# A fused two-block transformer kernel: the first modulation's products in turns with the norm's square sums, and the first dense tile in turns with the gates' products

## The chip, the cores and the metric

One core of a Trainium2 chip runs the whole program. The metric is the device time of one execution in microseconds, the median of three runs; lower is better. The engines are TensorE (PE in the rows; PEld is its weight loads), VectorE (DVE), ScalarE (ACT), GpSimd (POOL) and SyncE (SP), whose queue starts nearly all loads.

## The reference

Two blocks follow each other on 256 tokens of width 1024; the change lies in the first forty to seventy microseconds, at the start of the first block:

```python
mod = jax.nn.silu(c) @ w_ada[l] + b_ada[l]                  # 1024 -> 6 x 1024
sh1, sc1, g1, sh2, sc2, g2 = jnp.split(mod, 6, axis=-1)
h = modulate(x, norm1_g[l], sh1, sc1)                       # rms_norm(x, g) * (1 + sc1) + sh1
proj = h @ w_in[l]
q_a, k_a, v_a, qk_m, v_m, o_m, gates = jnp.split(proj, offs, axis=-1)
qa = rope(split_heads(q_a, ATT_HEADS), positions)           # sines and cosines of the positions
...
qk_m = jax.nn.silu(causal_conv(qk_m, conv_w[l], conv_b[l]))
gates = gates.astype(jnp.float32) + b_gate[l].astype(jnp.float32)
...
hm = mlstm_chunkwise(..., i_pre, f_pre)                     # uses the gates and qk_m, v_m
y = jnp.concatenate([attn.astype(x.dtype), hm], axis=-1) @ w_out[l]
x = x + g1[:, None, :] * y
...                                                         # 32 experts, then the second block
```

## The kernel before

Activations lie transposed: a tile is 128 features by 256 tokens, and `xT`, `hT` are eight of them. A dense product (`dense_t`) loads 1 MB of weights into a tile `w`, splits each half into a rounded part `whi` (ScalarE, line 267) and a rest `wlo` (VectorE, line 268), does the same to the activations (`hh`, `hl`), and adds three products for each of 8 feature blocks (`mm3`): 24 matmuls for a half, 48 for a whole block. All matmuls come from line 280.

The function `first` begins with the norm (`rstd`: ScalarE squares a block of `xT` into a tile `ats`, TensorE sums it over the features), then the sines and cosines of the positions (`sincos`: eleven short operations on VectorE and ScalarE from the load `posi`), then the modulation (`ada`): eight loads of 1 MB of `wada`, each with four matmuls against `crep`, a copy `m` on ScalarE, four transposes and one addition into `mod`. Three groups of `mod` are made; group 0 is needed at once, groups 1 and 2 (`more`) are taken one step after each dense block. From `mod` come `a1` and, block by block, `hh`, `hT` and `hl`; then the gates' products (`wg` against `hT`, eight matmuls of 36 columns of weights), the function `gates`, and four dense blocks for `qk_m`, each copied from the PSUM to a tile `raw` and then convolved.

The order on each engine isn't the order of the code. A scheduler works it out when the program is built, from the order of the code, the buffers that are free and its own estimate of each instruction's time; each engine then executes its list in that order. `tc.issue_after(x)` puts the instructions that are written under it, on the engine of `x`, behind `x`, without a wait on a semaphore. What limits the scheduler here: the pool `raw` holds five 1 MB tiles `w`, so a sixth load starts only when the first is used; the pool of `whi` and `wlo` holds four halves of each; `ps` has two PSUM banks, and one of them is held by the modulation group under way (`psum_banks(ps=2, at=3, ml=2, kv=1)`).

Of the kernel before, what the change touches and what calls it, by code (L numbers as in the profile page):

```python
# [3 lines left out]

# [1 line left out]

# [9 lines left out]
AF = mybir.ActivationFunctionType  # L16
OP = mybir.AluOpType
# [164 lines left out]
def bc(ap, n):  # L182

    return ap[:, None, :].to_broadcast([ap.shape[0], n, ap.shape[1]])
# [23 lines left out]
class Kern:  # L208
# [55 lines left out]

    def split(self, src, hi, lo, eng=None):

        self.nc.scalar.activation(hi, src, AF.Copy)  # L267
        (eng or self.nc.vector).tensor_sub(lo, src, hi.bitcast(F32))  # L268
        return hi, lo

# [6 lines left out]
            yield self.split(raw[:, 1024 * i:1024 * i + 1024], hi, lo, self.nc.gpsimd if i < self.spread else None)  # L277

    def mm(self, ps, l, r, start, stop, **kw):
        self.nc.tensor.matmul(ps, l, r, start=start, stop=stop, **kw)  # L280

    def mm3(self, ps, l, r, start, stop, **kw):

        self.mm(ps, l[0], r[0], start, False, **kw)
        self.mm(ps, l[0], r[1], False, False, **kw)
        self.mm(ps, l[1], r[0], False, stop, **kw)

    def dense_t(self, src, act, other=iter(())):

# [70 lines left out]
    def sincos(self, pool, ang, n, tag, tmp=None, out=None):  # L360

        nc = self.nc
        MAGIC = 12582912.0
        c1 = 6.28125
        c2 = float(np.float32(np.round((2 * PI - c1) * 2 ** 21) / 2 ** 21))
        c3 = float(np.float32(2 * PI - c1 - c2))
        k, r = (self.t(tmp[0], [128, n], tmp[1]) if tmp else self.t(pool, [128, n], tag + i) for i in "kr")
        s, c = out or [self.t(pool, [128, n], tag + i) for i in "sc"]
        nc.vector.tensor_scalar(k, ang, 1.0 / (2 * PI), MAGIC, op0=OP.mult, op1=OP.add)
        nc.vector.tensor_scalar(k, k, MAGIC, None, op0=OP.subtract)  # L370
        nc.vector.scalar_tensor_tensor(r, k, -c1, ang, op0=OP.mult, op1=OP.add)
        nc.vector.scalar_tensor_tensor(r, k, -c2, r, op0=OP.mult, op1=OP.add)
        nc.vector.scalar_tensor_tensor(r, k, -c3, r, op0=OP.mult, op1=OP.add)
        lim = 3.1415925
        nc.vector.tensor_scalar(r, r, -lim, lim, op0=OP.max, op1=OP.min)
        nc.scalar.activation(s, r, AF.Sin)
        nc.vector.scalar_tensor_tensor(k, r, -1.0, r, op0=OP.mult, op1=OP.max)
        nc.scalar.activation(c, k, AF.Sin, bias=self.halfpi, scale=-1.0)
        return s, c


# [22 lines left out]
    def ada(self, pool, g, crep):  # L404

        nc = self.nc
        ps = self.psum()
        for k in range(8):
            w = self.load(self.io["wada"][g, k])
            for j in range(4):  # L410
                self.mm(ps[32 * j:32 * j + 32], crep[:, k], w[:, 512 * j:512 * j + 512], k == 0, k == 7)
            yield
        m = self.t(pool, [128, 512], "ats")
        nc.scalar.activation(m, ps, AF.Copy)
        pt = self.psum().rearrange("p (q j r) -> p j q r", q=4, j=4)
        for q in range(4):
            nc.tensor.transpose(pt[:, :, q].rearrange("p j r -> p j r"), m[:, 128 * q:128 * q + 128], self.ident)
        dst = self.mod[:, 16 * g:16 * g + 16].rearrange("p (j q) -> p j q", j=4)
        b = self.v("b_ada", 16 * g, 16).rearrange("p (j q) -> p j q", j=4)
        nc.vector.tensor_add(dst, pt[:, :, :, 0], b)  # L420
# [16 lines left out]
    def first(self, M):  # L437
        nc, io, tc = self.nc, self.io, self.tc
        with tc.tile_pool(name="p1", bufs=1) as P, tc.tile_pool(name="p1w", bufs=2) as W:
            sc = self.t(P, [128, 8], "sc")  # L440
            nc.scalar.activation(sc, self.v("c"), AF.Silu)
            crep = self.t(P, [128, 8, 32], "crep")
            nc.vector.tensor_copy(crep, sc[:, :, None].to_broadcast([128, 8, 32]))
            C = self.load_c(P, ["cmask", "tneg", "rot", "hsel", "invf"])

            r1, _ = self.rstd(W, self.xT, "cv", sq="ats")
            hT = self.slot(0).rearrange("p (a b) -> p a b", a=8)
            nc.vector.tensor_mul(hT, self.xT, bc(r1, 8))
            posi = self.t(W, [128, T], "cv", I32)
# [13 lines left out]
            nc.vector.tensor_copy(ang, posi)  # L463
            nc.vector.tensor_scalar(ang, ang, C["invf"], None, op0=OP.mult)
            self.sincos(P, ang, T, "rp", (W, "cv"), (sinT, cosT))
            for _ in self.ada(W, 0, crep):
                pass
            more = itertools.chain(self.ada(W, 1, crep), self.ada(W, 2, crep))
            a1 = self.t(P, [128, 8], "a1")
            nc.vector.scalar_tensor_tensor(a1, self.m(1), 1.0, self.v("norm1_g"), op0=OP.add, op1=OP.mult)  # L470
            hh = self.t(P, [128, 8, T], "hh", F32R)
            hl = self.t(P, [128, 8, T], "hl", F32R)
            for k in range(8):
                nc.scalar.activation(hh[:, k], hT[:, k], AF.Identity, bias=self.mod[:, k:k + 1], scale=a1[:, k:k + 1])
                nc.vector.tensor_scalar(hT[:, k], hT[:, k], a1[:, k:k + 1], self.mod[:, k:k + 1], op0=OP.mult, op1=OP.add)
                nc.vector.tensor_sub(hl[:, k], hT[:, k], hh[:, k].bitcast(F32))
            h = (hh, hl)
            self.out("h", hT)
            wg = self.t(P, [128, 8, 36], "wg")
            nc.sync.dma_start(wg, io["wgate"][0])  # L480
            bg = self.t(P, [36, 1], "bg")
            nc.sync.dma_start(bg, io["bgate"])
            pg = self.psum("ml")[0:36, :T]
            for k in range(8):
                self.mm(pg, wg[:, k], hT[:, k], k == 0, k == 7)
            self.gates(P, C, pg, bg, hn, so)

            qkm = self.slot(1).rearrange("p (a b) -> p a b", a=8)
            for b in (0, 2, 1, 3):
                ps = self.dense_t(io["win"][4 + b], h)  # L490
                next(more, None)
                raw = next(raws)
                nc.scalar.activation(raw, ps, AF.Copy)
                for c in range(2):
                    f = 2 * b + c
                    cv = qkm[:, f]
                    wc = self.v("conv_w", 4 * f, 4)
                    nc.vector.tensor_scalar(cv, raw[:, c], wc[:, 3:4], self.v("conv_b", f), op0=OP.mult, op1=OP.add)
                    for d in (1, 2, 3):
                        nc.vector.scalar_tensor_tensor(cv[:, d:], raw[:, c, :T - d], wc[:, 3 - d:4 - d], cv[:, d:],  # L500
                                                       op0=OP.mult, op1=OP.add)
                if b >= 2:
                    for x in (qkm[:, 2 * b - 4:2 * b - 2], qkm[:, 2 * b:2 * b + 2]):
                        nc.scalar.activation(x, x, AF.Silu)
                    nc.gpsimd.tensor_scalar(x, x, 128.0 ** -0.5, None, op0=OP.mult)
            nc.vector.memset(vm[:, :, :, 128:132], 1.0)
            for b in range(2):
                ps = self.dense_n(io["winv"][2 + b], h)
                next(more, None)
                nc.scalar.activation(vm[:, :, 2 * b:2 * b + 2, 0:128], ps.rearrange("p a (h d) -> p a h d", h=2), AF.Copy)  # L510
            self.mlstm(W, C, qkm, vm, hn, CT, mE)

# [4 lines left out]
            for b in range(2):  # L517
                for s, o in enumerate((qT, kT)):
                    ps = self.dense_t(io["win"][2 * s + b], h)
# [3 lines left out]
                    pr = self.psum().rearrange("p (a b) -> p a b", a=2)  # L523
                    self.mm(pr, C["rot"], raw, True, True)
                    nc.vector.tensor_mul(t1, pr, bc(sinT, 2))
                    nc.gpsimd.tensor_mul(raw, raw, bc(cosT, 2))
                    nc.vector.tensor_add(o[:, 2 * b:2 * b + 2], t1, raw)
                ps = self.dense_n(io["winv"][b], h)
                next(more, None)
                nc.scalar.activation(va[:, :, 256 * b:256 * b + 256], ps, AF.Copy)  # L530
                for f in (2 * b, 2 * b + 1):
                    self.attention(W, C, f, qT, kT, va, ao, ss, next(pT0))
                if b == 0:
# [3 lines left out]
            for b in range(2):  # L537
                ps = self.dense_t(io["win"][8 + b], h)
# [30 lines left out]

    def gates(self, P, C, pg, bg, hn, so):  # L570

# [1270 lines left out]
```

## Time and profile before

| | |
|---|---|
| Median of three runs (lowest to highest) | 1499.58 us (1497.99 to 1507.75) |
| The profiled execution: its time, its span | 1499.36 us, 1497.3 us |
| Busy share of the span: PE, DVE, ACT, POOL | 89%, 51%, 37%, 22% |
| Mean granted TensorE clock | 0.93 |
| Moved by DMA | 414.86 MB, mean 277 GB/s |

The span is the profiled part of the execution; 2.06 us lie outside it. Busy shares are averages over stages with different limits: what the change is worth has to be read from the stage in which it lies. The clock column of a stretch is the share of TensorE's full clock (2.4 GHz) that was granted; 0.50 is its lower level, 1.2 GHz.

### The profile page before, as it was taken

The page shows a single profiled execution, that of the slowest core. Times are in us where ns is not written, and L with a number is a line of the kernel's source. Part 1 is how long each engine was busy: PE and PEld are TensorE (multiplying, and loading weights), DVE is VectorE, ACT ScalarE, POOL GpSimd, SP SyncE. Part 2 cuts the span into 40 slices and gives each one's busy share as a digit, 9 for nine tenths or more (in the row PEclk, how much of TensorE's full clock was granted, in tenths as well). Part 3 has the DMA queues.
Part 4 walks back from the last instruction along what each step waited for, and adds up shares of the span by engine and source line. Part 5 has one row for each costly group of instructions (what it writes and reads, how often), then busy time and mean ns, then how long its engine had stood idle before and what let it go on. Part 6 is the DMA issues. An engine that isn't in the chain of part 4 may idle for free. (4 is left out here: it accounts for less than half of the span.)

```text
span 1497.3 us, 25797 instructions
## 1 busy us (share of the span) xinstructions
PE 1337.9 (89%) x10632; PEld 1065.1 (71%) x10632; DVE 761.6 (51%) x1498; ACT 549.8 (37%) x859; POOL 323.3 (22%) x450
## 2 busy tenths in 40 slices
PE   5999998987887888686679999999999999999997
PEld 2777796553454555341159989999888988999997
DVE  2766454812233321010047686588846899665553
ACT  3754553321211122110034435644522355444443
POOL 0031121412223231200008887111400000030001
PEclk8899999998988999896689999999999999999998
DMA  9776764999999999999994525889766534675540
GB/s 364 277 268 250 268 246 174 379 400 420 420 408 415 420 408 420 420 421 374 421 370 156 204 92 178 259 251 320 265 203 204 170 138 147 213 205 189 178 141 29
DMA packets 87626, 414.86 MB, mean 277 GB/s; under 512 B 26432, under 2 KB 28016, under 8 KB 43472
## 3 DMA queue, kind: packets, MB, share of 16 engines
q1 hardware_dynamic: 66768, 381.85, 66.9%
q0 software_dynamic: 8016, 22.13, 4.7%
q10 hardware_dynamic: 12720, 9.18, 1.9%
q8 instruction: 86, 1.41, 0.4%
q14 instruction: 36, 0.29, 0.1%
HBM read 392.90 MB, written 20.22 MB: 276 GB/s over the span
## 5 line engine op out<-in xcount | busy, mean ns | idle before, releaser
L267 ACT ACTIVATE whi<-w 128x1024 fp32r<-128x1024 f32 x252 | 263.7, 1056 | 329.8 <-PE ps L280 249.9
L268 DVE TENSOR_TENSOR wlo<-w,whi 128x1024 fp32r<-128x1024 f32 x222 | 273.4, 1240 | 145.2 <-ACT whi L267 144.6
L280 PE MATMUL ps<-hh,whi 128*128 128x256 f32 x928 | 272.8, 294 | 11.2 <-DVE zt L1614 5.0
L280 PE MATMUL ps<-hh,wlo 128*128 128x256 f32 x928 | 266.9, 288 | 2.0 <-DVE wlo L268 1.8
L280 PE MATMUL ps<-hl,whi 128*128 128x256 f32 x928 | 267.8, 289 | 0.9 <-DVE hl L1579 0.7
L280 PEld LDWEIGHTS ps<-hh,whi 128*128 128x128 f32 x928 | 179.0, 193 | 19.5 <-issue 9.1
L280 PEld LDWEIGHTS ps<-hh,wlo 128*128 128x128 f32 x928 | 178.8, 193 | 4.5 <-DVE wlo L268 2.6
L280 PEld LDWEIGHTS ps<-hl,whi 128*128 128x128 f32 x928 | 179.0, 193 | 2.0 <-DVE hl L1579 0.7
L280 PE MATMUL A<-w,xg 128*32 128x512 f32 x984 | 139.6, 667 | 33.8 <-DMA w<-in_w 32.9
L280 PE MATMUL acc<-gyl,whi 128*128 128x256 f32 x384 | 109.1, 284 | 0.6 <-DVE gyl L268 0.6
L280 PE MATMUL acc<-gyh,wlo 128*128 128x256 f32 x384 | 109.1, 284 | 0.0
L280 PE MATMUL acc<-gyh,whi 128*128 128x256 f32 x384 | 108.2, 282 | 0.0
L268 POOL TENSOR_TENSOR wlo<-w,whi 128x1024 fp32r<-128x1024 f32 x30 | 70.6, 2368 | 167.1 <-ACT whi L267 166.9
L934 DVE SCALAR_TENSOR_TENSOR xT<-m,mod,xT 128x256 f32<-128x256 f32 x64 | 27.8, 480 | 142.7 <-PE m L280 142.7
L280 PEld LDWEIGHTS A<-w,xg 128*32 128x32 f32 x984 | 23.8, 114 | 102.3 <-DMA w<-in_w 73.2
L280 PE MATMUL A<-w,gT 128*32 128x512 f32 x512 | 75.0, 687 | 24.1 <-DMA w<-in_w 16.5
L960 DVE TENSOR_TENSOR g<-g,A 128x512 f32<-128x512 f32 x8 | 5.5, 687 | 134.3 <-PE A L280 134.3
L280 PEld LDWEIGHTS acc<-gyl,whi 128*128 128x128 f32 x384 | 72.7, 189 | 1.5 <-DVE gyl L268 0.8
L280 PEld LDWEIGHTS acc<-gyh,whi 128*128 128x128 f32 x384 | 73.2, 191 | 0.2 <-issue 0.2
L280 PEld LDWEIGHTS acc<-gyh,wlo 128*128 128x128 f32 x384 | 72.9, 190 | 0.2 <-issue 0.2
L1759 POOL TENSOR_TENSOR zs<-zs,yy 128x256 f32<-128x256 f32 x16 | 14.7, 935 | 236.9 <-DMA yy<-yd 236.1
L280 PE MATMUL ps<-wlo,hh 128*128 128x256 f32 x192 | 56.1, 292 | 3.4 <-DVE wlo L268 3.4
(585 smaller groups left out, 2766.8 us busy)
## 6 DMA issues: line engine op xcount, KB each, us to landing
w<-in_w SPq DMA_DIRECT2D x187, 1024.0 KB, 11.5
w<-in_wada SPq DMA_DIRECT2D x24, 1024.0 KB, 7.3
w<-in_wo SPq DMA_DIRECT2D x24, 1024.0 KB, 5.3
w<-in_sglu SPq DMA_DIRECT2D x16, 1024.0 KB, 4.9
w<-in_gz SPq DMA_DIRECT2D x12, 1024.0 KB, 6.9
w<-in_sz SPq DMA_DIRECT2D x12, 1024.0 KB, 4.8
w<-in_win SPq DMA_DIRECT2D x10, 1024.0 KB, 7.1
w<-in_xk SPq DMA_DIRECT2D x8, 1024.0 KB, 9.7
```

What stands on the lines that cost most here:

```text
L267: self.nc.scalar.activation(hi, src, AF.Copy)
L268: (eng or self.nc.vector).tensor_sub(lo, src, hi.bitcast(F32))
L280: self.nc.tensor.matmul(ps, l, r, start=start, stop=stop, **kw)
L934: self.nc.vector.scalar_tensor_tensor(self.xT[:, f], pc[:, T * c:T * c + T], self.m(5)[:, f:f + 1], self.xT[:, f], op0=OP.mult, op1=OP.add)
L960: nc.vector.tensor_mul(g1, g1, p3)
L1759: nc.gpsimd.tensor_mul(zs[:, f], zs[:, f], u)
```

## The change

Four things are written otherwise in `first`. The modulation's group 0 is started before the norm: each of its eight steps (load and four products) is followed by one square sum of the norm, and the load of the constants `c_cmask` comes at the fourth step. The rest of group 0 (copy, transposes, addition) stays behind the sines and cosines, and `issue_after(self.turn.ins)` puts its copy behind the last cosine on ScalarE. The first dense block is taken out of the loop: its first half's split is put behind `a1` on VectorE, the eight `hh` behind its `whi` on ScalarE, and its products for one feature block are followed by the gates' product for that block. The first products of groups 1 and 2 are put behind this block's last matmul. The core of the diff:

```diff
@@ ada @@
-            for j in range(4):
-                self.mm(ps[32 * j:32 * j + 32], crep[:, k], w[:, 512 * j:512 * j + 512], k == 0, k == 7)
+            with self.tc.issue_after(self.begun.ins) if g and k == 0 else nullcontext():
+                for j in range(4):
+                    self.mm(ps[32 * j:32 * j + 32], crep[:, k], w[:, 512 * j:512 * j + 512], k == 0, k == 7)
@@ first @@
-            C = self.load_c(P, ["cmask", "tneg", "rot", "hsel", "invf"])
-
-            r1, _ = self.rstd(W, self.xT, "cv", sq="ats")
+
+            ada = self.ada(W, 0, crep)
+            ps = self.psum()[:, :2].rearrange("p (t n) -> p t n", t=2)
+            for k in range(8):
+                next(ada)
+                if k == 3:
+                    C = self.load_c(P, ["cmask", "tneg", "rot", "hsel", "invf"])
+                self.square_sums(W, k, self.xT[:, k], self.cp["mean"][:, 0:1], ps, tag="ats")
+            r1 = self.rows(W, self.inv_root(W, ps[:, :, 0], "cvc"), "cv")
...
-            for _ in self.ada(W, 0, crep):
-                pass
+            with tc.issue_after(self.turn.ins):
+                for _ in ada:
+                    pass
...
+            block, ahead = self.psum().rearrange("p (a b) -> p a b", a=2), self.halves(io["win"][4])
+            with tc.issue_after(a1_.ins):
+                w0 = next(ahead)
             for k in range(8):
-                nc.scalar.activation(hh[:, k], hT[:, k], AF.Identity, bias=self.mod[:, k:k + 1], scale=a1[:, k:k + 1])
+                with tc.issue_after(self.hi.ins):
+                    nc.scalar.activation(hh[:, k], hT[:, k], AF.Identity, bias=self.mod[:, k:k + 1], scale=a1[:, k:k + 1])
...
-            for k in range(8):
-                self.mm(pg, wg[:, k], hT[:, k], k == 0, k == 7)
+            for c in range(2):
+                w = [x.rearrange("p (k m) -> p k m", k=8) for x in (w0 if c == 0 else next(ahead))]
+                for k in range(8):
+                    self.begun = self.mm3(block[:, c], [x[:, k] for x in w], [x[:, k] for x in h], k == 0, k == 7)
+                    if c == 0:
+                        self.mm(pg, wg[:, k], hT[:, k], k == 0, k == 7)
             self.gates(P, C, pg, bg, hn, so)
...
-                ps = self.dense_t(io["win"][4 + b], h)
+                ps = self.dense_t(io["win"][4 + b], h) if b else block
```

The built order shows what the scheduler made of it. It differs from the order before on TensorE down to its 288th matmul, on ScalarE down to its 64th instruction, on VectorE down to its 89th, and on SP in the first 48 loads; behind those points all lists are the same as before, and GpSimd's is the same throughout.

SP's queue at the start of the program, before (`c_ident`, `c_cmask`: constants; `cv<-in_pos`: the positions; `in_win`: the dense blocks' weights):

```order
L247 DMA c_ident<-in_cst 128x260
L390 DMA vec<-in_vec 128x184
L392 DMA xT<-in_xT 128x2048
L247 DMA c_cmask<-in_cst 128x1025
L262 DMA w<-in_wada 128x2048 x2
L450 DMA cv<-in_pos 128x256
L262 DMA w<-in_wada 128x2048 x6
L480 DMA wg<-in_wgate 128x288
```

SP's queue at the same place after the change:

```order
L247 DMA c_ident<-in_cst 128x260
L390 DMA vec<-in_vec 128x184
L392 DMA xT<-in_xT 128x2048
L262 DMA w<-in_wada 128x2048 x4
L247 DMA c_cmask<-in_cst 128x1025
L262 DMA w<-in_wada 128x2048 x4
L457 DMA cv<-in_pos 128x256
L482 DMA wg<-in_wgate 128x288
```

The constants `c_cmask` moved behind four of the eight loads of `wada`, and the load of the positions moved from behind the second of them to behind the eighth.

ScalarE from the modulation's copy (`ats<-ps`) to the gates' logarithm (`s_156<-s_156,c_ident`), before (`w<-ps` is the copy of a finished dense block):

```order
L414 ACTIVATE ats<-ps 128x512
L474 ACTIVATE hh<-s_151,mod,a_229 128x256 x8
L267 ACTIVATE whi<-w 128x1024 x4
L578 ACT_TABLE_LOAD
L578 ACTIVATE s_156<-s_156 4x256
L579 ACT_TABLE_LOAD
L579 ACTIVATE s_156<-s_156,c_ident 4x256
L493 ACTIVATE w<-ps 128x512
```

ScalarE at the same place after the change:

```order
L415 ACTIVATE ats<-ps 128x512
L267 ACTIVATE whi<-w 128x1024 x2
L490 ACTIVATE hh<-s_200,mod,a_229 128x256 x8
L267 ACTIVATE whi<-w 128x1024 x3
L510 ACTIVATE w<-ps 128x512
L595 ACT_TABLE_LOAD
L595 ACTIVATE s_205<-s_205 4x256
L267 ACTIVATE whi<-w 128x1024
L596 ACT_TABLE_LOAD
L596 ACTIVATE s_205<-s_205,c_ident 4x256
```

Two splits moved ahead of the eight `hh`, and the first dense block's copy moved ahead of the gates' exponential (L578, now L595).

TensorE at the transposes of the gates (`ml<-c_ident`), which stand in the second dense block, before, directly behind the four modulation products that follow the first block:

```order
L280 MATMUL ps<-w,crep 32x512 x4
L280 MATMUL ps<-hh,whi 128x256
L598 MATMUL ml<-c_ident,s_156 128x4
L280 MATMUL ps<-hl,whi 128x256
L598 MATMUL ml<-c_ident,s_156 128x4
L280 MATMUL ps<-hh,wlo 128x256
```

TensorE at the same transposes after the change, where 39 matmuls of the second block stand ahead of them, and the end of that block (`ml<-s_204,c_cmask` spreads the gates' running maximum over the partitions):

```order
L280 MATMUL ps<-hh,wlo 128x256
L615 MATMUL ml<-c_ident,s_205 128x4
L280 MATMUL ps<-hh,whi 128x256
L615 MATMUL ml<-c_ident,s_205 128x4
L280 MATMUL ps<-hl,whi 128x256
...
L280 MATMUL ps<-w,crep 32x512 x3
L280 MATMUL ml<-s_204,c_cmask 128x256 x2
L280 MATMUL ps<-w,crep 32x512
```

The transposes moved 38 matmuls further back, and the four products between the second and the third block are now three and one, with the gates' spreading between them.

## Rows read from the trace of the kernel before

**Rows 1.** SP's queue in order of time: start, duration, engine, line, operation.

```profile
3.75 0.63 SPq L450 DMA_DIRECT2D cv<-in_pos  x1
4.42 17.82 SPq L262 DMA_DIRECT2D w<-in_wada  x6
```

**Rows 2.** DMA from 8 to 20 us in 40 slices; second and third wada load, us to landing.

```profile
GB/s 437 437 410 410 410 437 437 437 437 437 410 437 437 246 120 75 82 102 113 290 372 416 410 413 447 410 410 437 437 382 410 437 437 410 410 437 437 437 437 410
...
w<-in_wada SPq DMA_DIRECT2D x1, 1024.0 KB, 10.9
...
w<-in_wada SPq DMA_DIRECT2D x1, 1024.0 KB, 13.8
```

**Rows 3.** Timeline, sincos and modulation: start, us, engine, line, operation, tiles, idle before.

```profile
19.74 0.29 DVE L463 CAST s<-cv 128x256 f32<-128x256 int32 x1
...
23.27 0.51 ACT L378 ACTIVATE s<-cv,c_ident 128x256 f32<-128x256 f32 x1
...
30.81 1.94 PE L280 MATMUL ps<-w,crep 128*32 128x512 f32 x8 [0.55 <-DMA w<-in_wada]
32.87 0.60 ACT L414 ACTIVATE ats<-ps 128x512 f32<-128x512 f32 x1 [9.09 <-PE ps L280]
...
34.88 0.17 DVE L470 SCALAR_TENSOR_TENSOR a<-mod,vec 128x8 f32<-128x8 f32 x1
```

**Rows 4.** Timeline from the modulation's end to the second dense block.

```profile
36.19 5.91 PE L280 MATMUL ml<-s,wg 128*36 128x256 f32 x14 [1.55 <-DVE s L475]
36.51 0.73 DVE L475 TENSOR_SCALAR s<-s,a,mod 128x256 f32<-128x256 f32 x2
...
37.82 0.73 DVE L475 TENSOR_SCALAR s<-s,a,mod 128x256 f32<-128x256 f32 x2
...
39.04 3.88 ACT L267 ACTIVATE whi<-w 128x1024 fp32r<-128x1024 f32 x4
...
40.78 1.21 DVE L268 TENSOR_TENSOR wlo<-w,whi 128x1024 fp32r<-128x1024 f32 x1
...
42.45 1.05 PE L280 MATMUL ps<-w,crep 128*32 128x512 f32 x2
...
42.94 1.28 ACT L578 ACT_TABLE_LOAD   x1
...
43.43 0.62 PE L280 MATMUL ml<-s,wg 128*36 128x256 f32 x2
...
43.98 0.38 PE L280 MATMUL ps<-hh,wlo 128*128 128x256 f32 x1
...
49.57 1.07 PE L280 MATMUL ps<-w,crep 128*32 128x512 f32 x8
```

**Rows 5.** Stretches: busy us (count) of PE, PEld, DVE, ACT, POOL; PEclk, DMA share, GB/s.

```profile
28.00:30.00 2.00, 1.68 (x8) 0.20 (x8) 0.00 (x0) 0.00 (x0) 0.00 (x0) 0.50 0.90 346
...
40.00:42.00 2.00, 2.00 (x6) 0.72 (x4) 2.00 (x5) 2.00 (x4) 0.00 (x0) 0.58 0.99 418
...
60.00:62.00 2.00, 2.00 (x11) 2.00 (x11) 0.49 (x2) 1.20 (x2) 0.00 (x0) 0.50 0.69 291
```

**Rows 6.** Timeline, two matmuls of a dense block at the lower clock.

```profile
60.40 0.41 PE L280 MATMUL ps<-hh,whi 128*128 128x256 f32 x1
60.61 0.41 PE L280 MATMUL ps<-hl,whi 128*128 128x256 f32 x1
```

**Rows 7.** Timeline, the gates' bias, logarithm and last difference before the transposes.

```profile
44.09 0.47 DVE L575 TENSOR_SCALAR s<-ml,bg 4x256 f32<-4x256 f32 x1 [1.76 <-PE ml L280]
...
48.39 0.51 ACT L579 ACTIVATE s<-s,c_ident 4x256 f32<-4x256 f32 x1
...
50.13 0.46 DVE L588 TENSOR_TENSOR s<-s 4x128 f32<-4x128 f32 x2
```

**Rows 8.** Stretches behind the change; columns as in Rows 5.

```profile
60.00:75.00 15.00, 15.00 (x116) 12.45 (x116) 11.35 (x24) 13.05 (x17) 1.49 (x1) 0.93 0.80 311
...
225.00:250.00 25.00, 19.25 (x152) 18.60 (x150) 17.33 (x59) 10.26 (x22) 6.75 (x4) 0.93 0.31 101
```

More of the change, by code (lines that the diff above doesn't have):

```diff
@@ L2 @@
 import math
-from contextlib import ExitStack
+from contextlib import ExitStack, nullcontext
 import numpy as np
@@ L265, in split @@
     def split(self, src, hi, lo, eng=None):
-        self.nc.scalar.activation(hi, src, AF.Copy)
+        self.hi = self.nc.scalar.activation(hi, src, AF.Copy)
         (eng or self.nc.vector).tensor_sub(lo, src, hi.bitcast(F32))
@@ L279, in mm @@
     def mm(self, ps, l, r, start, stop, **kw):
-        self.nc.tensor.matmul(ps, l, r, start=start, stop=stop, **kw)
+        return self.nc.tensor.matmul(ps, l, r, start=start, stop=stop, **kw)
     def mm3(self, ps, l, r, start, stop, **kw):
@@ L285, in mm3 @@
         self.mm(ps, l[0], r[1], False, False, **kw)
-        self.mm(ps, l[1], r[0], False, stop, **kw)
+        return self.mm(ps, l[1], r[0], False, stop, **kw)
     def dense_t(self, src, act, other=iter(())):
@@ L377, in sincos @@
         nc.vector.scalar_tensor_tensor(k, r, -1.0, r, op0=OP.mult, op1=OP.max)
-        nc.scalar.activation(c, k, AF.Sin, bias=self.halfpi, scale=-1.0)
+        self.turn = nc.scalar.activation(c, k, AF.Sin, bias=self.halfpi, scale=-1.0)
         return s, c
@@ L465, in first @@
             self.sincos(P, ang, T, "rp", (W, "cv"), (sinT, cosT))
-            for _ in self.ada(W, 0, crep):
-                pass
+            with tc.issue_after(self.turn.ins):
+                for _ in ada:
+                    pass
             more = itertools.chain(self.ada(W, 1, crep), self.ada(W, 2, crep))
             a1 = self.t(P, [128, 8], "a1")
-            nc.vector.scalar_tensor_tensor(a1, self.m(1), 1.0, self.v("norm1_g"), op0=OP.add, op1=OP.mult)
+            a1_ = nc.vector.scalar_tensor_tensor(a1, self.m(1), 1.0, self.v("norm1_g"), op0=OP.add, op1=OP.mult)
             hh = self.t(P, [128, 8, T], "hh", F32R)
             hl = self.t(P, [128, 8, T], "hl", F32R)
+            wg = self.t(P, [128, 8, 36], "wg")
+            nc.sync.dma_start(wg, io["wgate"][0])
+            bg = self.t(P, [36, 1], "bg")
+            nc.sync.dma_start(bg, io["bgate"])
+            block, ahead = self.psum().rearrange("p (a b) -> p a b", a=2), self.halves(io["win"][4])
+            with tc.issue_after(a1_.ins):
+                w0 = next(ahead)
             for k in range(8):
-                nc.scalar.activation(hh[:, k], hT[:, k], AF.Identity, bias=self.mod[:, k:k + 1], scale=a1[:, k:k + 1])
+                with tc.issue_after(self.hi.ins):
+                    nc.scalar.activation(hh[:, k], hT[:, k], AF.Identity, bias=self.mod[:, k:k + 1], scale=a1[:, k:k + 1])
                 nc.vector.tensor_scalar(hT[:, k], hT[:, k], a1[:, k:k + 1], self.mod[:, k:k + 1], op0=OP.mult, op1=OP.add)
@@ L478, in first @@
             self.out("h", hT)
[L479 to L482, printed above, removed]
             pg = self.psum("ml")[0:36, :T]
-            for k in range(8):
-                self.mm(pg, wg[:, k], hT[:, k], k == 0, k == 7)
+            for c in range(2):
[4 more added lines that the diff above has]
+                        self.mm(pg, wg[:, k], hT[:, k], k == 0, k == 7)
             self.gates(P, C, pg, bg, hn, so)
```

## The prediction

> **What bounds the kernel now.** I read the windows by stage first, then the timeline of the first 80 us, then SP's queue and the DMA slices. The change lies in the first 80 us, and all lists of instructions are the same behind it, so the question is by how much that stretch gets shorter, and whether the rest passes this on. It does: right behind the first block's mixer the DMA engines are busy for 0.31 of the time [rows 8], so the expert loads that follow wait for the engines and start earlier or later with them. A microsecond won or lost at the start is one at the end.
>
> In the first 31 us the loads of `wada` set the pace: TensorE waits for the last of them until 30.81, its four products take 1.94, and then copy, transposes, addition and `a1` follow one another, `a1` from 34.88 to 35.05 [rows 3]. The reader should see that sines and cosines, done at 23.78, are far from that chain before. From 36.19 TensorE runs the gates' products, seven of them in 5.91 us (the row counts two passes each, x14), so 0.845 us apiece, at the lower clock; the first dense block starts in earnest at 43.98 and its products are done at 49.57 [rows 4].
>
> **The loads.** The SP queue serves in the order of issue as far as the trace shows: `cv<-in_pos` was issued at 3.75, between the second and the third `wada` load [rows 1], and the DMA rate falls from about 425 GB/s to between 75 and 290 in the seven slices from 11.9 to 14.0 us, where those loads go through [rows 2]. Against 425 GB/s the seven slices lose 1.4 us. The landings say the same: the third load (4.42 + 13.8) landed at 18.2, about 4.1 us after the second, which was issued half a microsecond before the positions, where the last products start 2.5 us apart. So the positions cost 1.4 to 1.6 us of DMA time; I take 1.5. With this load behind the eighth `wada`, that one lands at 29.3 instead of 30.8. The constants' load moves too, but stays ahead of the last `wada` load: worth nothing. Nothing else holds the eighth load up: it needs the buffer of the third one, whose product the new order has right behind the eighth square sum, on a load that landed at 18.2 even before; its own bytes come no earlier than 26.8, one load of 2.5 ahead of 29.3.
>
> **The positions come last.** Now the positions' own bytes lie behind the eighth `wada`: they land at 29.3 (if they overlap it) to 31.4 (the 2.1 us for which the rate was low), and I take 30.8, one cost of 1.5 behind. From the cast of the positions to the end of the last cosine the trace has 19.74 to 23.78, 4.04 us, without a wait inside [rows 3]; VectorE and ScalarE execute in order, and the modulation's copy, by the new constraint, and its addition stand behind that chain. So the copy starts at 34.85 instead of 32.87, and `a1` ends at 37.05 instead of 35.05: the modulation is ready **2.0 us later** (0.5 to 2.6), although its products are done at 31.25, 1.5 us sooner. Here a rule of the Trainium skill speaks against the change. The page "DMA: Bandwidth & Descriptors" (Queues, rings and completion order) states that each DMA engine takes descriptors in ring order; by that rule the positions can't overtake the `wada` loads, as the trace has it, and without it this term would be nothing and the sum 1499.8.
>
> **The first dense block.** Behind the copy (0.60 us, to 35.45) ScalarE now runs two `whi`, 0.97 each [rows 4], to 37.4, so `hh` starts 0.35 us behind `a1`; VectorE runs one `wlo` of 1.21 first, to 38.26, then `hT` and `hl` in pairs, 1.31 us a pair (36.51 to 37.82, rows 4), so that the last is done at 43.5. TensorE has its first matmul at 37.95 and steady work from 38.6. The half block with the gates' products is 24 x 0.21 [rows 6] + 8 x 0.845 = 11.8 us at the lower clock, and 24 x 0.12 (46 matmuls from 43.98 to 49.57) + 8 x 0.55 (43.43 to 43.98) = 7.3 at the full one [rows 4]. TensorE comes out of a rest here as before, where the clock was at 0.50 from 28 us and rose at 41.7 (0.58 over 40 to 42, rows 5), 5.5 us after the gates' products began; with the same delay it rises at 43.45. By then 4.85 / 11.8 = 41% is done, and the other 59% takes 4.3: 47.75. The second half takes 24 x 0.12 = 2.9, the products of group 1 1.0, and the second dense block starts at 51.65, where before it was 49.57 + 1.0 = 50.6. So this part is **+1.0**: the overlap of dense and gates' products gives back 1.0 of the positions' 2.0.
>
> **The gates' chain.** Before, the bias started at 44.09, the logarithm was done at 48.90, the values for the transposes at 50.6, 1.7 later [rows 7], just when TensorE began the second block: no wait. Now the bias can start when the gates' products end, 47.75, but on ScalarE the exponential stands behind the first block's copy. From the block's end at 50.65: copy 0.60 (the modulation's, of the same size, rows 3), table load 1.28 [rows 4], exponential about 0.5 (by the logarithm's row), `whi` 0.97, table load 1.28, logarithm 0.51: 55.8. Another 1.7 gives 57.5 for both chunks, somewhat less for the first one, 57.3. TensorE reaches the transposes after 39 matmuls of the second block, 51.65 + 4.7 = 56.35. It waits **1.0 us** (0 to 2), and behind it is all dense work.
>
> **The products of groups 1 and 2.** One product alone takes as long as four on four column groups: x2 in 1.05, x8 in 1.07 [rows 4]. Down to the 288th matmul the order before has seven such batches, the new one eight, because three and one are parted: **+1.0**, 0 if the lone product runs in a wait.
>
> **The clock in the second block.** Before, the clock fell to 0.50 around 60 us [rows 5], behind the gates' spreads, and 16 matmuls ran at 0.21 instead of 0.12: 1.4 us. The new order has the spreads 20 us into dense work and further apart: the dip goes (-1.4), stays (0), or comes twice (+1.4). I take half of it away, **-0.7**.
>
> The first fetch of expert weights, moved forward in SP's queue, falls into a stretch where TensorE is always busy and DMA at 0.80 [rows 8]. I cost it at nothing; if that cover is gone, it is 2.5 us, one load.
>
> **Sum.** +1.0 + 1.0 + 1.0 - 0.7 = +2.3 on the profiled execution's 1499.36, hence **1501.7**. That execution is 0.2 below the median of 1499.58; the three runs lie between 1497.99 and 1507.75, and about 1%, 15 us, is what a measurement of this kernel can tell from no change.
>
> **Rivals.** *The positions aren't last, and TensorE keeps its clock.* If the positions land with the eighth `wada`, all is 1.5 us earlier; if the turns of products and sums keep the clock at its full level, the half block takes 7.3 from 37.1, and the second block starts at 37.1 + 7.3 + 2.9 + 1.0 = 48.3, 2.3 us earlier than before. With the transposes' wait (+1.0) covered by that, the lone product (+1.0) and the dip (-0.7) this is -2.0: 1497.4. For it: TensorE is busy from 10 to 20 us without a rest. Against it: with a product every 2.5 us the clock was at 0.50 from 28 us before [rows 5], and TensorE rests from 31.25 to 35.5 now. The Trainium skill, "TensorE: Matmul & The Clock Gate" (Part 1), states that activity releases the clock and rest takes it back; what the turns do by that rule no row here shows. Chance 0.22.
>
> *More waits in the new order.* The positions land at 31.4 and the clock dips twice: +0.6 and +2.1 on the sum, 1504.4. Chance 0.18.
>
> *The clock doesn't come back* (the other side). The first block's matmuls wait for VectorE pair by pair, and if TensorE is too little active for the clock to rise before the loop of dense blocks and the gates' waits keep it down, the 168 dense matmuls from 43 to 79 us pay 0.09 each, 15.1 us, and eight product batches 0.9 each, 7.2: some +24 with the sum, 1524. It ends over 1% slower if it holds for the better half of that stretch. Against it: before, the clock rose within 5.5 us on gates' products alone [rows 5]. Chance 0.03.
>
> **How the numbers follow.** The forecast has 0.53; 0.02 each is left for gains and losses from a place I haven't looked at. The range takes the first two rivals in with a run's spread of some 1 us: 1496.5 to 1505.5, 8 in 10 or a little more. Over 1% faster, only the unseen: 0.02. Over 1% slower, the clock: 0.03. Within 1%: 0.95.
>
> **What would show it.** The cast of the positions starts near 30.8 after a wait on VectorE that ends with their load (right before 29.5: no loss there); the last `wada` product starts at 29.3; `a1` ends near 37; the clock rises near 43.5; the second block starts near 51.6; TensorE waits near 56 for the gates' transposes. From 85 us on every instruction should stand 1 to 4 us later than before, the same to the end. Wrong I am if the positions' load comes out of the queue early, if the clock never falls before 38, or if a later stage doesn't pass the shift on.

## The result, and the profile after

The changed kernel takes **1508.0 us** (median of 22 runs, 1503.7 to 1515.3), the kernel before 1500.0 in the same series (22 runs, 1495.5 to 1507.8): ratio 1.0052, 95% interval 1.004 to 1.0063, so 6.0 to 9.4 us slower. The forecast was 1501.7 in a range of 1496.5 to 1505.5: the sign was right, the size about a third of what came. The profiled execution took 1504.71, with a span of 1502.7. Ratios and intervals, here and below, compare fast runs of one series with each other (one run of 2422.5 us, of the last kernel below, is left out of its ratio), and they differ from the quotient of the two medians by up to 0.002, or 3 us.

The timeline of the changed kernel, with SP's queue (columns as in [rows 1, 3]):

```profile
23.59 0.43 SPq L457 DMA_DIRECT2D cv<-in_pos  x1
...
31.03 0.29 DVE L470 CAST s<-cv 128x256 f32<-128x256 int32 x1 [3.98 <-DMA cv<-in_pos]
...
34.99 0.58 ACT L415 ACTIVATE ats<-ps 128x512 f32<-128x512 f32 x1
...
36.98 0.17 DVE L478 SCALAR_TENSOR_TENSOR a<-mod,vec 128x8 f32<-128x8 f32 x1
...
44.10 0.28 PE L280 MATMUL ps<-hh,wlo 128*128 128x256 f32 x1
...
46.31 0.28 PE L280 MATMUL ps<-hh,wlo 128*128 128x256 f32 x1
46.52 0.62 PE L280 MATMUL ml<-s,wg 128*36 128x256 f32 x2
47.07 0.39 PE L280 MATMUL ps<-hh,whi 128*128 128x256 f32 x1
47.30 0.28 PE L280 MATMUL ps<-hl,whi 128*128 128x256 f32 x1
47.41 0.28 PE L280 MATMUL ps<-hh,wlo 128*128 128x256 f32 x1
47.62 0.62 PE L280 MATMUL ml<-s,wg 128*36 128x256 f32 x2
...
49.27 0.39 PE L280 MATMUL ps<-hh,whi 128*128 128x256 f32 x1
...
49.38 0.47 DVE L592 TENSOR_SCALAR s<-ml,bg 4x256 f32<-4x256 f32 x1 [3.55 <-PE ml L280]
...
52.28 1.07 PE L280 MATMUL ps<-w,crep 128*32 128x512 f32 x8
...
53.28 0.39 PE L280 MATMUL ps<-hh,whi 128*128 128x256 f32 x1
...
59.22 0.22 PE L615 MATMUL ml<-c_ident,s 4*128 4x4 f32 x1 [1.04 <-DVE s L605]
...
60.97 1.06 PE L280 MATMUL ps<-w,crep 128*32 128x512 f32 x6
...
63.01 1.05 PE L280 MATMUL ps<-w,crep 128*32 128x512 f32 x2
...
72.68 1.90 PE L280 MATMUL ps<-w,crep 128*32 128x512 f32 x10
...
80.35 1.92 PE L280 MATMUL ps<-w,crep 128*32 128x512 f32 x14
...
82.46 1.05 PE L280 MATMUL ps<-w,crep 128*32 128x512 f32 x2
...
166.05 0.33 SPq L262 DMA_DIRECT2D w<-in_xk  x1
```

The positions' load is issued behind the eight `wada` loads, and VectorE waits 3.98 us for it; the copy (34.99) and `a1` (36.98) come 2.1 later than in [rows 3]. In the dense block one feature block takes from 46.52 to 47.62 with the gates' product in turns. The bias stands 5.3 later than in [rows 7], the product batch behind the first block 2.7 later than in [rows 4]. TensorE waits at the transposes, and the four products are parted into three (x6) and one (x2), each batch as long as four; at 82.46 another product stands alone. The last line is the mark used below: the load of `in_xk`, far behind the changed stretch, is issued at 162.12 in the profile read for the forecast.

The windows of the changed kernel (columns as in [rows 5]):

```profile
33.00:42.00 9.00, 5.04 (x15) 2.93 (x15) 6.63 (x19) 7.84 (x14) 0.00 (x0) 0.55 0.99 418
42.00:50.00 8.00, 8.00 (x36) 4.41 (x36) 4.43 (x9) 2.34 (x3) 0.00 (x0) 0.87 0.42 145
50.00:60.00 10.00, 8.96 (x72) 7.63 (x71) 8.32 (x20) 6.96 (x8) 0.00 (x0) 1.00 0.75 289
60.00:75.00 15.00, 15.00 (x96) 10.37 (x97) 9.96 (x25) 11.08 (x14) 1.63 (x1) 1.00 0.71 235
```

The clock comes back in the window from 42 to 50 and then stays at 1.00, where the kernel before had a dip [rows 5, 8].

### The profile page after: what moved, and what is told of

Same layout as the page of the kernel before. It is cut to its first block, busy times and chain, and to the rows that moved or that the text cites. A ratio compares the mean times of both kernels' runs of the same rounds, so it can differ in the third digit from the quotient of the medians.

```text
span 1502.7 us, 25796 instructions
## 1 busy us (share of the span) xinstructions
PE 1345.6 (90%) x10632; PEld 1065.4 (71%) x10632; DVE 760.9 (51%) x1498; ACT 550.4 (37%) x860; POOL 323.7 (22%) x450
## 5 line engine op out<-in xcount | busy, mean ns | idle before, releaser
L280 PE MATMUL A<-w,xg 128*32 128x512 f32 x984 | 143.0, 681 | 34.5 <-DMA w<-in_w 33.7
```

Of the source, the lines that this page charges most:

```text
L280: return self.nc.tensor.matmul(ps, l, r, start=start, stop=stop, **kw)
```

## The experiments

**One profile is one draw.** Both kernels were profiled again, unchanged: the changed one three times more, the kernel before three times more. Of the changed kernel's second profile the medians were taken too.

> The changed kernel itself, once more, beside the kernel before on the same chip. First theory (the end gets what the start loses, microsecond for microsecond): its fifth dense block started 4.6 us later than before, so it ends 4 to 6 us later, ratio 1.003 to 1.004. Second theory (a later stage makes the loss larger): 7 to 9 us later, ratio 1.005 to 1.006, as the medians had it.

> The kernel before, unchanged, profiled once more: how much of a difference between two profiles is the execution and not the kernel. The mark is the load w<-in_xk, issued at 162.12 in the profile that the prediction read and at 166.05 and 165.29 in two profiles of the changed kernel. First theory (one profile is a fair picture of the start): it stands at 161.6 to 162.6 again, and the stretch from there to the last issue lasts 1327.8 give or take 2. Second theory (the profile that was read had an unlucky start, with its clock dip near 60 us, and a lucky rest): the mark stands at 160 to 161, and the rest lasts 1330 or more.

> The same once more, with the same expectations: mark at 161.6 to 162.6 by the first theory, 160 to 161 by the second.

> The changed kernel, a third profile. If the start alone makes the loss, w<-in_xk stands at 165 to 166.5 as in the first two; if some executions lose more in the dense blocks (the clock falls behind the wait for the transposes), at 168 or later.

> The same, a fourth: 165 to 166.5 by the first theory, 168 or later by the second.

> The kernel before, a fourth profile: w<-in_xk at 158.5 to 162.2, the ends of the three so far; earlier or later if these do not show the spread.

Starts in us, with the mean of each four in the last row of a kernel:

| kernel | `a1` | second dense block | `w<-in_xk` | last issue | time |
|---|---|---|---|---|---|
| before, as read | 34.88 | 50.57 | 162.12 | 1489.91 | 1499.36 |
| before | 34.60 | 49.39 | 160.26 | 1495.74 | 1504.74 |
| before | 32.81 | 47.85 | 158.69 | 1487.36 | 1496.57 |
| before | 33.59 | 48.48 | 159.98 | 1501.22 | 1510.37 |
| mean | 33.97 | 49.07 | 160.26 | 1493.56 | |
| changed | 36.98 | 53.28 | 166.05 | 1495.07 | 1504.71 |
| changed | 36.98 | 52.52 | 165.29 | 1497.54 | 1506.83 |
| changed | 36.73 | 52.53 | 166.06 | 1496.58 | 1506.46 |
| changed | 35.65 | 51.93 | 165.40 | 1500.77 | 1510.30 |
| mean | 36.59 | 52.57 | 165.70 | 1497.49 | |

In the second series the changed kernel is 1.0066 of the kernel before (1.0041 to 1.0091; medians 1507.69 and 1500.65), which fits the second theory better than the first. Of the two new theories on the kernel before the first fell, and the second held in part: the profile that was read had the slowest start of the four, but in the third the start is sooner than 160 and the rest, 1328.7, shorter than the 1330 that it asked for. All four marks of the changed kernel stand where the theory of a loss at the start had them, none at 168. The third profile of the kernel before shows how the start can be sooner:

```profile
30.07 1.06 PE L280 MATMUL ps<-w,crep 128*32 128x512 f32 x8 [1.07 <-DMA w<-in_wada]
...
32.81 0.17 DVE L470 SCALAR_TENSOR_TENSOR a<-mod,vec 128x8 f32<-128x8 f32 x1
...
47.85 0.39 PE L280 MATMUL ps<-hh,whi 128*128 128x256 f32 x1
...
158.69 0.33 SPq L262 DMA_DIRECT2D w<-in_xk  x1
```

Its last four modulation products start 0.7 sooner than in [rows 3] and take 1.06 instead of 1.94: there TensorE ran at the full clock, in the profile read at the lower one. Against the mean of four the changed kernel loses 165.70 - 160.26 = **5.4 us** up to the mark, and its four marks lie within 0.8 of each other; those of the kernel before lie within 3.4, so the 5.4 is uncertain by some 2 us. The difference is all there by the end of the changed stretch: compared matmul by matmul, the means of four stand 5.4 apart at 82 us and 5.3 to 5.5 apart from there to the mark. From the mark to the last issue the kernel before takes 1327.8 to 1341.2 (mean 1333.3), the changed one 1329.0 to 1335.4 (mean 1331.8): no loss is to be seen there, but the spread of 13 us within one kernel would hide one of several us.

**Does a late start end late?** The kernel before with two useless loads of 1 MB ahead of the modulation's:

```diff
+            for i in (1, 2):
+                nc.sync.dma_start(self.slot(i), io["wada"][0, i])
             C = self.load_c(P, ["cmask", "tneg", "rot", "hsel", "invf"])
```

> The kernel before, with two loads of 1 MB that nobody needs put ahead of its constants and its modulation's loads; every other instruction is the same and in the same order on each engine. At 410 to 437 GB/s these two take about 4.9 us, so the modulation and all dense blocks stand some 4.9 us later. First theory: the end is 4 to 6 us later too, 1503 to 1506. Second theory (growth in a later stage, by the ratio of 7.8 to 4.6): 7.5 to 9 us later, 1507.5 to 1509. A third theory (the growth comes from the new order of the first 75 us and not from the shift) expects here what the first does.

```profile
37.02 0.60 ACT L414 ACTIVATE ats<-ps 128x512 f32<-128x512 f32 x1 [13.50 <-PE ps L280]
...
164.60 0.33 SPq L262 DMA_DIRECT2D w<-in_xk  x1
```

The modulation's copy starts 4.9 us later than the mean of the four (32.87, 32.59, 31.26, 31.58), the mark 4.3 later, and the end 5.7 (1506.33 against 1500.65; 1.0041, 1.0021 to 1.0061). So a start that is late by some 4 us ends late by about as much; growth by a factor of 1.7 is neither needed nor quite excluded. Start and mark are those of one profile here.

**What the positions' load costs.** In the changed kernel the tile of the positions is filled from 128 different rows:

```diff
-            nc.sync.dma_start(posi, io["pos"].to_broadcast([128, T]))
+            nc.sync.dma_start(posi.bitcast(F32), io["cst"][:, 0:T])
```

> The changed kernel with one load altered: the tile of the positions is filled from a table of the same size whose 128 rows are different ones, instead of one row of 1 KB read 128 times. The sines and cosines, and so the rotated queries and keys, are of other numbers. All orders are those of the changed kernel. My theory (128 reads of one row hold the DMA up for 1.5 to 2 us): the cast of the positions starts 1.2 to 1.8 us sooner than the 31.03 of the changed kernel, a1 and the second dense block likewise, and the end is 1 to 2 us sooner than the changed kernel's. Rival (the dip in the DMA rate is the queue running empty before the next loads, whatever is read): the cast starts at 30.7 to 31.1 as before.

Busy share in tenths and rate of DMA from 20 to 36 us, in 40 slices, of the changed kernel and then of this one:

```profile
DMA  9999998999999899989987899999899899999999
GB/s 471 410 410 451 389 451 369 471 410 410 451 389 369 307 410 471 430 369 292 156 61 73 98 293 367 373 427 483 369 410 451 369 430 471 389 410 471 410 410 451
```

```profile
DMA  9998999999899899979999999989999999999999
GB/s 410 430 451 369 410 492 389 410 430 451 369 410 492 369 430 430 410 292 356 430 418 430 430 389 389 451 369 430 451 389 430 410 451 410 430 410 410 430 410 451
```

The engines are busy in both, but 128 reads of one row bring the rate down to 61 GB/s for about 2 us; with different rows the dip is gone, so the rival fell. The cast starts at 28.27 instead of 29.7 to 31.0, `a1` at 34.21 (2.4 before the mean), the mark is issued at 162.69 (3.0 before it). So by this one profile 2.4 of the 2.6 us that `a1` loses against the kernel before are these reads in that place. The time shows little of the gain: 1506.83, against 1507.69 of the changed kernel in the same series, and against the kernel before 1.006 (1.0038 to 1.0082), where its start, 2.4 behind that kernel, would give 1.0016. With six and seven runs that are spread over 8 us the gain of 3 can neither be seen nor excluded in the times; that they are so far above 1.0016 stays unexplained.

**The halves, and two repairs.** First the second half of the change alone, then the first half, then the changed kernel with the first block's copy behind the gates' logarithm, and with the positions' load first:

```diff
 (third)
+                with tc.issue_after(self.ln.ins):
+                    nc.scalar.activation(raw, ps, AF.Copy)
 (fourth)
+            posi = self.t(W, [128, T], "cv", I32)
+            nc.sync.dma_start(posi, io["pos"].to_broadcast([128, T]))
             ada = self.ada(W, 0, crep)
```

> The second half of the change alone: norm, positions and modulation as in the kernel before, then the first dense block in turns with the gates' products, as in the change. My theory, by the trace of the changed kernel: a1 ends at 35.05 as before; from there to the second dense block the changed kernel takes 16.1 to 16.3 (37.15 to 53.28), the kernel before 15.5, and the wait for the gates' transposes (1.3) and the parted product batch (1.0) come on top: 2 to 3 us later at the load w<-in_xk, and 2 to 4 at the end. Rival: the turns cost nothing by themselves and all of the loss hangs on the positions' load: within 1 us of the kernel before.

> The first half of the change alone: products and square sums in turns, constants' and positions' loads later, the modulation's copy behind the last cosine; gates' products and first dense block are left to the scheduler as in the kernel before. My theory: a1 ends at 37.0 to 37.2, 2.1 later than before, since the positions' load lies behind the eighth load; w<-in_xk and the end are 1.5 to 3 us later. Rival (a delay at the start is hidden behind the dense blocks' own loads, and only the second half of the change costs): within 1 us of the kernel before at that mark.

> The changed kernel with the first dense block's copy put behind the gates' logarithm on ScalarE, where the change has it ahead of the exponential. My theory: TensorE no longer waits for the gates' transposes (1.04 by the wait, 1.3 of pause in the changed kernel), the load w<-in_xk comes at 164 to 165 (165.3 and 166.1 in the changed kernel), end 1 to 2 us sooner than the changed kernel, 1506 to 1507. Rival (the scheduler plans 402 of TensorE's matmuls anew from there, and the new order has waits of its own, as in the two halves alone): w<-in_xk at 168 or later, end 1510 or more.

> The whole change with the load of the positions ahead of the eight loads of the modulation instead of behind them. My theory (the positions' place makes the modulation late): the last cosine and the copy behind it stand 3 us sooner than the changed kernel's 34.57 and 34.99, a1 at 33.1 to 33.3, the second dense block at 49 to 49.5, w<-in_xk at 161.5 to 162.5, end 1 to 2 us later than the kernel before. Rival (the dense block in turns costs by itself): the second dense block at 51 or later. Second rival (the scheduler plans 615 of TensorE's matmuls otherwise than in the kernel before, and the new order is worse in itself, as in the two halves): w<-in_xk at 168 or later, end 1510 or more.

| | `w<-in_xk` | median, before | ratio (interval) |
|---|---|---|---|
| second half alone | 172.36 | 1511.53, 1501.66 | 1.0053 (1.0033 to 1.0073) |
| first half alone | 173.97 | 1511.58, 1501.66 | 1.0077 (1.0052 to 1.0102) |
| gates ahead of the copy | 174.20 | 1512.97, 1499.88 | 1.0074 (1.0056 to 1.0092) |
| positions first | 172.46 | 1511.74, 1499.88 | 1.0064 (1.0047 to 1.0081) |

All four lose 12 to 14 us at the mark, more than the whole change, and my theory fell in each; in the last two the rival that a new order costs by itself came true. What they share is that the scheduler planned 400 to 615 of TensorE's matmuls anew, where the change as it was made moves 287. TensorE's longest wait from 50 to 165 us in the second half alone (what waits, for what: us, times, longest), and the windows of the kernel with the gates ahead:

```profile
PE ml L280 <- DVE s L718: 5.4, 1, 5.4
```

```profile
55.00:60.00 5.00, 4.04 (x18) 3.55 (x19) 4.45 (x14) 1.60 (x3) 0.00 (x0) 0.65 0.99 392
60.00:65.00 5.00, 5.00 (x16) 3.47 (x16) 1.40 (x6) 1.85 (x4) 0.00 (x0) 0.50 0.93 383
65.00:70.00 5.00, 5.00 (x20) 4.61 (x20) 1.70 (x3) 4.04 (x5) 0.00 (x0) 0.50 0.02 8
70.00:75.00 5.00, 5.00 (x29) 4.00 (x28) 0.75 (x4) 2.15 (x4) 0.00 (x0) 0.64 0.00 2
```

The wait ends at 120 us in the mixer of the block; the first half alone and the kernel with the positions first have one of 4.9 and 4.8 in that place, the changed kernel 0.5. With the gates ahead TensorE rests 2.39 us for the block's copy, up to 55.97, and the clock is at its lower level from 60 to 70; over 60 to 75 it is 0.77, 0.77 and 0.68 in the other three, 1.00 in the changed kernel. So these kernels tell of other orders, not of the parts of the change, and the split into halves stays untested; what each part costs is read from the profiles of the change itself, further down. In the last one the modulation was indeed ready early (`a1` at 33.39), and the second block still started at 52.44.

**The turns of products and sums, with the positions first,** and the first dense block as before (parts of the difference to the changed kernel):

```diff
+            posi = self.t(W, [128, T], "cv", I32)
+            nc.sync.dma_start(posi, io["pos"].to_broadcast([128, T]))
             ada = self.ada(W, 0, crep)
 ...
-            with tc.issue_after(a1_.ins):
-                w0 = next(ahead)
 ...
-                ps = self.dense_t(io["win"][4 + b], h) if b else block
+                ps = self.dense_t(io["win"][4 + b], h)
```

> The modulation's products and the square sums in turns and the constants later, as in the change, but the load of the positions ahead of all eight loads and no constraint on the modulation's copy; the first dense block as before the change. Behind the 31st of 8969 TensorE instructions all orders are those of the kernel before. My theory: the turns of products and sums are worth nothing, since the eighth load sets the pace: last product at 30.8, a1 at 34.9, end within 1.5 us of the kernel before. The rival (a buffer's release or the square sums' waits hold the loads up): last product later than 32, end 2 us or more later.

`a1` starts at 33.08, the mark at 159.89, the time is 1498.88 against 1500.65 (0.9988, 0.9969 to 1.0007). As expected, the turns in themselves cost nothing that the time shows, and the last product starts at 30.10 (expected 30.8); `a1` is 1.8 sooner than expected, within the spread of the kernel before. Here all orders behind the first thirty matmuls are the old ones. (The constraint that puts the modulation's copy behind the last cosine is in this kernel and in those of one row with products and sums in turns, other than the expectation says: the copy follows the cosine at 31.54 here.)

**Positions as one row.** One row of 1 KB is loaded, and one TensorE product spreads it over the partitions; first in the kernel before, then with products and sums in turns, and the latter once more:

```diff
-            posi = self.t(W, [128, T], "cv", I32)
-            nc.sync.dma_start(posi, io["pos"].to_broadcast([128, T]))
+            posi = self.t(P, [1, T], "posi", I32)
+            nc.sync.dma_start(posi, io["pos"])
+            posf = self.t(P, [1, T], "posf")
+            nc.vector.tensor_copy(posf, posi)
 ...
+            pp = self.psum("ml")[:, :T]
+            self.mm(pp, self.cp["cols"][0:1, 2:3].to_broadcast([1, 128]), posf, True, True)
+            nc.vector.tensor_scalar(ang, pp, C["invf"], None, op0=OP.mult)
```

> The kernel before with one thing altered: the positions are loaded as one row of 1 KB, made into numbers there and spread over the partitions by one TensorE product, instead of a load that reads the row 128 times. All other instructions stand in the order of the kernel before. My theory (the 128 reads of one row hold all DMA up for 1.5 to 2.8 us, and the modulation waits for the load behind them): a1 ends at 31.0 to 33.4, where three profiles of the kernel before have 32.98 to 35.05; end 1.5 to 3 us sooner than before, ratio 0.998 to 0.999. Rival (the eighth load's pace hangs on TensorE's clock and the release of buffers, not on that load): a1 at 33 to 35 and no difference at the end.

> The same load of one row, with the modulation's products and the square sums in turns and that load ahead of them (no part of the change behind the modulation). My theory: as with the positions first and 128 reads (a1 at 33.08 there), less the 1.5 to 2.8 us of the reads: a1 at 30.5 to 31.7 if TensorE's work in turns allows it, end 2 to 4 us sooner than the kernel before. Rival: the square sums and the sines, which end at 31.6 there behind TensorE's turns, set a1, and nothing is won: a1 at 32.5 to 33.3.

> The load of one row with products and sums in turns once more, for its interval: by its start (w<-in_xk at 157.5 against a mean of 160.4 in the kernel before) 2 to 4 us sooner than before, ratio 0.997 to 0.999; if its first measurement was a lucky draw, no difference.

In the kernel before this wins nothing: 1500.62 against 1499.88 (0.9997, 0.9983 to 1.0011), with `a1` at 35.44, later than even the rival had it. Its timeline, and DMA from 16 to 24 us in 40 slices:

```profile
17.73 8.02 PE L280 MATMUL ps<-w,crep 128*32 128x512 f32 x48
28.82 1.51 PE L280 MATMUL ps<-w,crep 128*32 128x512 f32 x8 [3.07 <-DMA w<-in_wada]
...
35.44 0.17 DVE L473 SCALAR_TENSOR_TENSOR a<-mod,vec 128x8 f32<-128x8 f32 x1
```

```profile
DMA  9989999799799799642100099069769969979999
GB/s 492 451 369 410 451 410 451 328 532 451 328 532 410 328 492 451 287 164 82 82 41 41 0 246 205 0 164 287 287 246 451 451 287 573 410 328 532 410 287 246
```

Now the busy share falls with the rate, down to 0: the engines had nothing to do. The five buffers `w` were full, and the sixth load had to wait for the modulation's first products, which stand behind the square sums and begin at 17.73. The rival was right that the buffers hold the loads up. The reads of one row seem to have hidden this wait: in the kernel before the rate has no dip in these 8 us (mean 424 GB/s, 325 here). In turns with the sums the buffers come free sooner, and both together win. The timeline of the first of the two runs:

```profile
30.20 0.58 ACT L415 ACTIVATE ats<-ps 128x512 f32<-128x512 f32 x1
...
31.73 0.17 DVE L481 SCALAR_TENSOR_TENSOR a<-mod,vec 128x8 f32<-128x8 f32 x1
...
46.56 0.38 PE L280 MATMUL ps<-hh,whi 128*128 128x256 f32 x1
...
157.46 0.33 SPq L262 DMA_DIRECT2D w<-in_xk  x1
```

The mark is at 157.46 and, in the second run, at 158.47, 1.8 to 2.8 before the mean of the kernel before; the times are 1497.49 against 1499.88 (0.9981, 0.996 to 1.0002) and 1498.21 against 1500.98 (0.9974, 0.996 to 0.9988). The second interval excludes that there is no gain, the first just fails to: some 2 to 4 us **better than both kernels**. How much of it the one row adds to the turns is not shown: with the turns and 128 reads the interval was 0.9969 to 1.0007, and `a1`, at 33.08 there, is at 31.73 and 32.83 here.

## Why the prediction was wrong, step by step

**Right.** *The loads*: the last `wada` products start at 29.2 in the second profile of the changed kernel and are done by 30.3 in the first (forecast 29.3 and 31.25). *The positions come last*: cast at 29.7 to 31.0 (30.8), behind the last `wada` load in all four profiles. This agrees with the Trainium skill, "DMA: Bandwidth & Descriptors" (Queues, rings and completion order), by which each DMA engine takes its descriptors in ring order. (Without this term the forecast's sum is 1499.7, not 1499.8.) The modulation's copy stands behind the cosine, and `a1` is 2.6 later than the mean of the kernel before (2.0, bounds 0.5 to 2.6). *The gates' chain*: TensorE waits 1.04 at the transposes in all four profiles (1.0), 0.6 to 1.9 us later than said. *The dip of the clock* goes, in whole and not by half. The first rival fell: the positions were last, and the clock was at 0.50 to 0.55 from 33 to 42.

**The step that failed is "The first dense block"**, which was to give back 1.0 of the positions' 2.0. From the start of `a1` to the second block the changed kernel takes 15.98 (mean of four), the kernel before 15.10: it costs another 0.9. Two errors meet in it. One is the price of the half block in turns. In the profile above 41% of it were done when the clock rose, as forecast, but that was at 44.1 instead of 43.45; the other 59% took 5.17 (44.10 to 49.27) instead of 4.3, and the second half 0.1 more than the 2.9: together the 1.6 by which the second block came later than 51.65. The 0.9 in the middle is the price of a turn: I charged a gates' product and three dense matmuls with 0.55 + 3 x 0.12 = 0.91 at the full clock, and the timeline has 1.10 (46.52 to 47.62), since the first dense matmul behind a gates' product starts the next one only after 0.23, and the change back costs 0.1 as well; five turns were left. In the other three profiles the clock rose 1.4 to 1.7 sooner (0.96 to 0.98 over 42 to 50), in one of them behind an `a1` that was itself 1.3 sooner, so the stretch varies from 15.5 to 16.3. The other error is the base: the profile that I read took 15.69 here, 0.6 more than the mean.

**A gain that was taken twice.** "The products of groups 1 and 2" counted seven batches before and eight after (a batch is one to four products side by side, about 1 us), which is right for the whole stretch. But of the seven, two stand ahead of the second block, the lone product at 42.45 and the four at 49.57 [rows 4], and of the eight only one, at 52.28. Behind it the kernel before, in the profile that was read, has these:

```profile
62.34 1.92 PE L280 MATMUL ps<-w,crep 128*32 128x512 f32 x14
...
70.02 1.06 PE L280 MATMUL ps<-w,crep 128*32 128x512 f32 x8
...
76.97 1.90 PE L280 MATMUL ps<-w,crep 128*32 128x512 f32 x10
```

A row of more than four products (x10, x14) is two batches, so five follow here, and seven in the changed kernel (60.97, 63.01, 72.68, 80.35, 82.46): two more and not one. The first dense block's sum had already kept the gain, its 51.65 without a lone product against 50.6 with one. So the 1.0 that I took for the worth of the overlap was this product, put off until later, and behind the block +2.0 was due where the sum has +1.0.

**The sum by its terms**, forecast and then measured against the mean of four at the mark: positions +2.0, +2.6; first dense block -1.0, +0.9; what follows it (gates' chain 1.0, batch 1.0, dip -0.7) +1.3, +1.95 (from the second block to the mark 113.13 against 111.19). Together +2.3, **+5.4**. The dip of the clock does go: it is in all four profiles of the kernel before (0.94 over 50 to 60 and 0.93 over 60 to 75 in the one read, 0.83 and 1.00 in the others) and in none of the changed kernel. So that gain was -1.4, twice what I took; with the wait of 1.0 and two batches more for 2.0 this makes 1.6 of the 1.95, and some 0.3 has no name.

**"A microsecond at the start is one at the end"** held as far as the times can tell: +5.4 at the mark against +6.0 to +9.4 in the medians, and 4.3 against 3.1 to 9.2 with the useless loads. From 85 us on I expected 1 to 4 us; against the profile read it was 3.2 to 4.6, and that profile's start was itself 1.9 later than the mean. Whether the 2 us or so between 5.4 and the medians are a loss further back or the spread of the starts, these runs do not show.

The third rival, the clock that doesn't come back, did not happen to the changed kernel. A relative of it happened to four kernels close to it: their clock rose before 50 us and fell again, for 7 to 17 us of the stretch from 50 to 75. What made it fall there is not shown.

## What to carry to other kernels

Profile the kernel before more than once ahead of a sum of 1 or 2 us: here its start varied by 3.4 us between executions, more than the whole forecast, while its total looked typical. A transfer's place in a queue and its price are two things; ask, when it gets cheaper, which buffer or which wait stands right behind it. Work that leaves one stretch has to be charged in the stretch in which it turns up. And where a scheduler orders the work, a half of a change is not half of its effect: compare the built orders, and trust an experiment on a part only where everything else stays in its place.

## What the runs showed of the hardware

- A load of 128 KB that reads one row of 1 KB 128 times kept the DMA engines busy in a dip of about 2 us, down to 61 to 98 GB/s for 1.2 of them, where the same tile from 128 rows went through at 292 to 451; `a1` stood 2.4 us sooner without it (one profile, against the mean of four).
- Low DMA rates had two faces here: engines busy at 0.7 to 0.9 or more at 61 to 98 GB/s (one row read again and again), and engines down to 0 (no buffer free).
- The time at which TensorE's clock rises differs between executions of one kernel: the last four modulation products took 1.94 us in one and 1.06 in another, and the second dense block started 2.7 us apart, 0.7 of which the products' own start made.
- Plain and rounded products in turns cost about 0.2 us a turn at the full clock on top of the products themselves (1.10 against 0.91).
- A rest of TensorE of 2.4 us that ended at 56 us was followed by a granted clock of 0.65 over 55 to 60 and 0.50 from 60 to 70, where TensorE was busy without a pause.
